# Hybrid decoder trunk: the later convolution's product and taps written behind the gate group's first subtraction

## The chip, the cores and the metric

The kernel runs on one core of a Trainium2 chip. The core has five engines that run side by side and wait for each other through semaphores: TensorE (PE, matmuls into the accumulation banks PSUM), VectorE (DVE), ScalarE (ACT), GpSimd (POOL) and SyncE (SP). DMAs are issued from the queues of SyncE, ScalarE and GpSimd. The metric is the time of the whole kernel in device microseconds; 1647.53 us is the median of three runs of the kernel before (1644.74 to 1648.75).

## What is computed

Two layers (D_MODEL 2048, 512 tokens, float32). Each normalises the input, projects it once into all heads, mixes in three branches and projects back:

```python
h = _rmsnorm(x, norm_g)
proj = h @ w_in
y_conv = _short_conv(cv_h, cv_b, cv_c, conv_w, conv_b) * silu(cv_g)   # b * (conv3(c * h) + bias)
...                                                                  # stick-breaking attention, linear attention
mix = jnp.concatenate([y_conv, y_sb, y_gla], axis=-1)
return x + mix @ w_out
```

The change concerns the first branch: the product c * h, and the causal convolution of width 3 over the tokens, which is done with three taps per channel.

## The kernel before

**Column groups.** The input projection is cut into groups of 256 columns, listed in `specs`, and worked off in that order; `cursor` counts them. The convolution has 512 channels, done as two convolutions of 256: conv 0 early in the layer, conv 1 last of all input groups. Each has four groups, in the order h, c, g, b. Behind "conv b 1" come the eight groups of the output projection.

**Weights.** `fetch(i)` (L362) loads a group's 2 MB of weights into one of two staging buffers `st`, from GpSimd's queue. ScalarE takes sums of squares (L383), GpSimd adds them over the partitions (L399), and VectorE makes a scale of them (L402 to L417). The weights are then split into a high and a low half in 16 bits: for a plain group ScalarE makes `wh` (L454) and VectorE `wl` (L461), in two halves of the depth. Each product is three matmuls: high by high, high by low, low by high.

**Quick groups.** The groups named in `QUICK_IN`, "conv c 1" and "conv g 1" among them, are done by `project_quick` with seven products of quarter blocks instead of eight. Their seven weight sums are made in `wsums` (L507 on ScalarE, L508 on VectorE; the seventh pair is `w7h`, `w7l`). The products go into two banks: pa and pb in one, pd and pf in the other, 24 matmuls each; in code order w11, wT2, w22, wT3, w21, wt1, wT4, where wT4 is the seventh weight and adds to pd. Between them ScalarE copies a partial result (L808, L812, L815) and VectorE adds and subtracts (L809, the first subtraction, then L816 to L821). wT4 may start only when L812 has read pd.

**conv 1.** `conv_in(1, go)` projects h into `hb` (L1198) and c into `uc`, multiplies c by its scale and by `hb` (L1203, once for each 128 channels, in place in `uc`), and makes `y` with the last tap and the bias (L1213) and the two earlier taps (L1215). `conv_out` projects the gate (group g) with `project_gate`, multiplies `y` by it (L1222), takes the largest value for a scale (`weight_ratio`), projects b with `project_cols` (L701 to L703) and multiplies by that (L1237).

**What stands beside it.** The last attention pair ends at the same time, spread out through `go`: `scores(1)` makes the weights of four query blocks (scans L1280, L1282), splits them (L1285 on ScalarE, L1286 on VectorE) and sends them through DMA transposes on SyncE's queue (L1288); `values` multiplies them with v (L1304) and applies the gate (L1308). `mixload` loads the finished parts of the mix back from DRAM (L923), the high half and then the low half, also on SyncE's queue; `weight_ratio` then brings all parts to one scale (L1188 on ScalarE, L1189 on VectorE), and the first output group multiplies them (L712 to L714).

**What sets the order.** The kernel is written through a scheduler that simulates the engines and puts each engine's instructions in the order in which they get ready there, by priority and by the place in the code. `order(a, b)` ties a behind b in that order without a wait on the chip. Only the opening of the kernel is in an order written by hand.

Of the kernel before, what the change touches and what calls it, by code (L numbers as in the profile page):

```python
# [11 lines left out]
ALU = mybir.AluOpType  # L12
# [31 lines left out]
def hybrid_trunk(ctx, tc, x, norm_g, w_in, conv_w, conv_b, sb_qn_g, sb_kn_g,  # L44
# [132 lines left out]
    def pcol(k, i):  # L177
        return par[:, base[k] + i:base[k] + i + 1]
# [506 lines left out]
    for l in range(depth):  # L685
# [89 lines left out]
                parts.extend([a[:, 2 * n], a[:, 2 * n + 1]] for n in range(2))  # L775
            return sums_of((xh, xl), parts, lambda t: [wk([P, HK, P], tag) for tag in ("zw", "zw", "g")])

        def project_quick(src, sums, y, cols):

            (w11, wT2, w22, wT3, w21, wt1, wT4), u = weights()  # L780
            (pa, pb), (pd, pf) = ([bk[:, n * GW:(n + 1) * GW] for n in range(2)]
                                  for bk in [bank(psp, "p") for _ in range(2)])
            a11, a12, a22 = ([a[:, 2 * r:2 * r + 2, c::2, :] for a in src] for r, c in ((0, 0), (0, 1), (1, 1)))
            s_, a21_22, a12_s, a11_21 = sums

            def prod(o, w, a, start, stop=False):
                for t in range(1 if cols else 2):
                    for kk in range(HK):
                        for i, (p_, q_) in enumerate(((0, 0), (0, 1), (1, 0))):
                            st_ = start and t == kk == i == 0  # L790
                            en = stop and kk == HK - 1 and i == 2
                            if cols:
                                mm = T.matmul(o, w[q_][:, kk, :], a[p_][:, :, kk, :], start=st_, stop=en,  # L793
                                              skip_group_check=True)
# [12 lines left out]
            hook(prod(pb, wT2, s_, False))  # L807
            S.activation(y12, za, AF.Copy)  # L808
            V.tensor_tensor(y21, zb, y12, ALU.subtract)  # L809
            prod(pf, w22, a12_s, True)  # L810
            prod(pd, wT3, a11_21, False)
            S.activation(y22, zd, AF.Copy)  # L812
# [3 lines left out]
            V.tensor_tensor(y12, zb, y12, ALU.subtract)  # L816
# [7 lines left out]
        def project(cols, dst):  # L824
# [4 lines left out]
            for _, u in project_quick((xh, xl), insums, y, cols):  # L829
                pass  # L830
            if cols:
                return [y[:, c, :] for c in range(2)], u
            return [y[:, 2 * b:2 * b + 2, :].rearrange("p a c -> p (a c)") for b in range(2)], u
# [13 lines left out]
                ps.append(o)  # L847
                yield t, o, u

        def project_gate(mx=None, logistic=False, room=None):  # L850
# [7 lines left out]
            ps, u = project(True, dst)  # L858
            quick_ = bool(g)
            g = dst() if not quick_ else g[0]  # L860
            top = sm(2, "gtop2") if mx is not None else None
            for c in range(2):
                y = g[:, c, :]
                if logistic:
                    a = wk([P, seq], "ga") if quick_ else y
                    tables.append(S.activation(a, ps[c], AF.Sigmoid, scale=u))
                    for b in tables[-9:-1]:
                        order(tables[-1], b)
                    if mx is None:
                        V.scalar_tensor_tensor(y, ps[c], u, a, ALU.mult, ALU.mult)  # L870
# [322 lines left out]
        def conv_in(j, then=lambda: None):  # L1193
# [5 lines left out]
            then()  # L1199
            uc = wk([P, 2, seq], "raw", 1) if j else wk([P, 2, seq], "zw")  # L1200
            ps, u = project(True, lambda: uc)
            for c in range(2):
                V.scalar_tensor_tensor(uc[:, c, :], ps[c], u, hb[:, c, :], ALU.mult, ALU.mult)  # L1203
            if j:
                mixload()
            y = wk([P, 2, seq], "kT")
            for c in range(2):
                ch = 2 * j + c

                def w_(i):  # L1210
                    return pcol("cw", (l * 3 + i) * 4 + ch)

                V.tensor_scalar(y[:, c, :], uc[:, c, :], w_(2), pcol("cb", l * 4 + ch), ALU.mult, ALU.add)  # L1213
                for d in (1, 2):
                    V.scalar_tensor_tensor(y[:, c, d:], uc[:, c, :seq - d], w_(2 - d), y[:, c, d:], ALU.mult, ALU.add)  # L1215
            then()
            return y, None if j else hb

        def conv_out(j, y, room, then=lambda: None):

            g, u = project_gate(logistic=j == 1, room=room)
            V.tensor_tensor(y, y, g, ALU.mult)  # L1222
            bound = sm(2, "cm")

# [249 lines left out]
```

## Time and profile before

| | |
|---|---|
| runs | 1644.74, 1647.53, 1648.75 us (median 1647.53) |
| profiled execution, its own time | 1652.09 us |
| its span, first to last instruction | 1650.3 us |
| TensorE busy | 1624.0 us (98%) |
| VectorE busy | 1418.1 us (86%) |
| ScalarE busy | 1184.7 us (72%) |
| granted TensorE clock | 1.0 |

The span is what the profile's times count from; the execution's own time is 1.8 us more. In a timeline a row gives the start, the duration, the engine, the line of the kernel, the operation with output and input, and in brackets how long the engine had been idle and what ended that. Matmuls overlap: a row's duration is longer than the distance to the next.

### The profile page before, as it was taken

What the parts mean: (1) busy time and instruction counts of PE and PEld (TensorE: products, weight loads), DVE (VectorE), ACT (ScalarE), POOL (GpSimd) and SP (SyncE); (2) the same over time, 40 slices, a digit from 0 to 9 for tenths busy, and PEclk for the clock granted to TensorE, in tenths of its full rate; (3) what the DMA queues carried; (4) which work ended last, traced back from release to release, by engine and by line L of the source; (5) the groups of instructions that cost most, each with busy time, mean ns of one, the idle gap of its engine ahead of it and who ended that gap; (6) DMA issues with size and microseconds to landing.
All of it is one profiled execution on the core that took longest, in us unless ns stands there. A gap on an engine that the chain in (4) does not pass through costs nothing.

```text
span 1650.3 us, 41605 instructions
## 1 busy us (share of the span) xinstructions
PE 1624.0 (98%) x17914; PEld 1342.5 (81%) x17914; DVE 1418.1 (86%) x2377; ACT 1184.7 (72%) x1743; POOL 265.8 (16%) x298
## 2 busy tenths in 40 slices
PE   8999999999999999999999999999999999999999
PEld 6746668989999967799986468689898989668998
DVE  7977989989898978898699689898898889888893
ACT  7667887877777776756766687787777768666571
POOL 0121011111112121111112011221121111211110
PEclk9999999999999999999999999999999999999999
DMA  7144334486768687544633344445776886894441
GB/s 259 54 146 127 73 113 100 116 161 149 166 148 167 148 167 207 161 154 150 204 110 116 103 116 112 132 94 137 152 157 153 151 163 152 165 189 157 154 155 53
DMA packets 193913, 234.90 MB, mean 142 GB/s; under 512 B 90226, under 2 KB 154044, under 8 KB 193216
## 3 DMA queue, kind: packets, MB, share of 16 engines
q0 software_dynamic: 76992, 177.22, 40.5%
q1 hardware_dynamic: 107728, 45.56, 14.5%
q10 hardware_dynamic: 9008, 9.45, 1.7%
q8 instruction: 140, 2.29, 0.6%
q14 instruction: 45, 0.37, 0.1%
HBM read 179.65 MB, written 14.68 MB: 118 GB/s over the span
## 4 chain that ended last, share of the span: by engine, by line
PE 37%; DVE 6%; DMA 4%; ACT 2%; issue 1%; POOL 0%; SPq 0%; DVEq 0%; ACTq 0%; POOLq 0%
PE psp L796 10%; PE psp L793 6%; PE psp L843 5%; PE psp L712 3%; PE psp L714 3%; PE psp L713 3%; PE psp L701 2%; PE psp L702 2%; PE psp L703 2%; DMA st<-in_w_in_dram 2%; DVE wl L508 1%; DMA m<-mixd 1%; DMA th<-za 1%; DVE za L1280 1%; DMA kT<-raw 1%
## 5 line engine op out<-in xcount | busy, mean ns | idle before, releaser
L507 ACT ACTIVATE wh<-st,ws 128x1024 f16<-128x1024 f32 x252 | 280.8, 1145 | 174.5 <-DVE st L527 92.0
L508 DVE SCALAR_TENSOR_TENSOR wl<-st,ws,wh 128x1024 f16<-128x1024 f32 x252 | 316.7, 1278 | 31.1 <-ACT wh L507 31.0
L383 ACT ACTIVATE junk<-st 128x2048 uint8<-128x2048 f32 x150 | 285.4, 1903 | 17.9 <-DMA st<-in_w_in_dram 8.8
L793 PE MATMUL psp<-s,wh 128*128 128x256 f16 x1152 | 195.6, 273 | 0.0
L793 PEld LDWEIGHTS <-wh 128*128 128x128 f16 x1728 | 168.3, 98 | 21.5 <-issue 1.3
L796 PE MATMUL psp<-wh,s 128*128 128x128 f16 x2048 | 176.9, 219 | 1.9 <-issue 1.9
L714 PE MATMUL psp<-wh,m 128*128 128x256 f16 x640 | 174.5, 273 | 1.2 <-DVE m L1189 1.2
L712 PE MATMUL psp<-wh,m 128*128 128x256 f16 x640 | 174.5, 273 | 0.2 <-issue 0.2
L796 PEld LDWEIGHTS <-s 128*128 128x128 f16 x3072 | 172.9, 98 | 2.0 <-issue 2.0
L713 PE MATMUL psp<-wl,m 128*128 128x256 f16 x640 | 174.5, 273 | 0.0
L796 PE MATMUL psp<-wl,s 128*128 128x128 f16 x1024 | 173.2, 219 | 0.0
L461 DVE SCALAR_TENSOR_TENSOR wl<-st,ws,wh 128x2048 f16<-128x2048 f32 x68 | 158.9, 2346 | 14.6 <-ACT wh L454 13.8
L454 ACT ACTIVATE wh<-st,ws 128x2048 f16<-128x2048 f32 x66 | 130.5, 1995 | 40.7 <-DVE ws L415 22.6
L362 POOL DMA_DIRECT2D st<-in_w_in_dram x114 | 109.8, 1029 | 297.8 <-DVE w7l L508 110.7
L793 PE MATMUL psp<-s,wl 128*128 128x256 f16 x576 | 156.7, 273 | 0.0
L796 PEld LDWEIGHTS <-m 128*128 128x128 f16 x2304 | 131.1, 98 | 2.7 <-issue 2.2
L399 POOL PARTITION_ALL_REDUCE wgm<-wm x75 | 55.5, 740 | 482.5 <-ACT junk L383 469.4
L386 POOL DMA_DIRECT2D st<-st x34 | 54.0, 1589 | 307.2 <-ACT junk L383 266.8
L793 PEld LDWEIGHTS <-wl 128*128 128x128 f16 x864 | 84.5, 98 | 13.4 <-issue 3.4
L796 PE MATMUL psp<-wh,m 128*128 128x128 f16 x1024 | 91.5, 219 | 0.4 <-DVE kT L809 0.4
L796 PE MATMUL psp<-wl,m 128*128 128x128 f16 x512 | 87.5, 219 | 0.0
L703 PEld LDWEIGHTS <-wl 128*128 128x128 f16 x448 | 43.8, 98 | 53.6 <-DVE wl L461 2.3
(442 smaller groups left out, 4199.8 us busy)
## 6 DMA issues: line engine op xcount, KB each, us to landing
st<-in_w_in_dram POOLq DMA_DIRECT2D x114, 1024.0 KB, 8.3
st<-in_w_out_dram POOLq DMA_DIRECT2D x32, 1024.0 KB, 8.5
st<-st POOLq DMA_DIRECT2D x34, 512.0 KB, 6.8
st<-in_w_in_dram SPq DMA_DIRECT2D x6, 1024.0 KB, 12.0
mixd<-g POOLq DMA_DIRECT2D x20, 256.0 KB, 7.9
x<-in_x_dram SPq DMA_DIRECT2D x4, 1024.0 KB, 4.9
qT<-in_x_dram ACTq DMA_DIRECT2D x8, 512.0 KB, 6.2
qT<-xs ACTq DMA_DIRECT2D x8, 512.0 KB, 4.0
```

The costliest lines, as they stand in the source:

```text
L362: load = queue.dma_start(s_, src[l, h * HK * P:(h + 1) * HK * P, c0:c0 + GW].rearrange("(k p) n -> p k n", p=P), max_dma_last_dim=1024)
L383: sq = S.activation(junk(HK * GW).rearrange("p (k n) -> p k n", k=part.shape[1]), part, AF.Square, accum_out=peak[i][:, h:h + 1])
L454: hi = S.activation(wh[:, :, :GW], staged[i][h], AF.Copy, scale=scales[i])
L461: V.scalar_tensor_tensor(wl[:, :, :GW], staged[i][h], scales[i], wh[:, :, :GW], ALU.mult, ALU.subtract)
L507: hi = S.activation(h_, b, AF.Copy, scale=sc)
L508: V.scalar_tensor_tensor(l_, b, sc, h_, ALU.mult, ALU.subtract)
L712: T.matmul(o, ah[:, t, k, :], wh[:, kk, :n], start=st_, stop=False, skip_group_check=True)
L713: T.matmul(o, ah[:, t, k, :], wl[:, kk, :n], start=False, stop=False, skip_group_check=True)
L714: return T.matmul(o, al[:, t, k, :], wh[:, kk, :n], start=False, stop=en, skip_group_check=True)
L793: mm = T.matmul(o, w[q_][:, kk, :], a[p_][:, :, kk, :], start=st_, stop=en, skip_group_check=True)
L796: mm = T.matmul(o[:, t * P:(t + 1) * P], a[p_][:, t, kk, :], w[q_][:, kk, :], start=st_, stop=en, skip_group_check=True)
L843: mm = T.matmul(o[:, :n], a_[:, t, k, :], w[k // HK][part][:, k % HK, :n], start=i == 0 and k == 0, stop=i == 2 and k == KT - 1)
```

## The change

For conv 1 alone, the product L1203 and the taps are put into a function `taps`, which `project_quick` calls through `mid` right behind the first subtraction L809 of the gate group, and the product is tied behind that subtraction. conv 0 calls `taps` where the code stood. Lines behind the change shift by 2 to 19 (L809 keeps its number; L1203 becomes L1210, L1213 L1219, L1215 L1221).

```diff
@@ -775,7 +775,7 @@
-        def project_quick(src, sums, y, cols):
+        def project_quick(src, sums, y, cols, mid=None):
...
@@ -806,7 +806,9 @@
             S.activation(y12, za, AF.Copy)
-            V.tensor_tensor(y21, zb, y12, ALU.subtract)
+            a = V.tensor_tensor(y21, zb, y12, ALU.subtract)
+            if mid is not None:
+                mid(a)
             prod(pf, w22, a12_s, True)
...
@@ -1199,26 +1201,43 @@
             then()
             uc = wk([P, 2, seq], "raw", 1) if j else wk([P, 2, seq], "zw")
             ps, u = project(True, lambda: uc)
-            for c in range(2):
-                V.scalar_tensor_tensor(uc[:, c, :], ps[c], u, hb[:, c, :], ALU.mult, ALU.mult)
             if j:
                 mixload()
-            y = wk([P, 2, seq], "kT")
-            for c in range(2):
-                ch = 2 * j + c
...
-            then()
-            return y, None if j else hb
+
+            def taps(behind=None):
+                y = wk([P, 2, seq], "kT")
+                for c in range(2):
+                    a = V.scalar_tensor_tensor(uc[:, c, :], ps[c], u, hb[:, c, :], ALU.mult, ALU.mult)
+                    if behind is not None:
+                        order(a, behind)
+                for c in range(2):
+                    ch = 2 * j + c
...
+                    V.tensor_scalar(y[:, c, :], uc[:, c, :], w_(2), pcol("cb", l * 4 + ch), ALU.mult, ALU.add)
+                    for d in (1, 2):
+                        V.scalar_tensor_tensor(y[:, c, d:], uc[:, c, :seq - d], w_(2 - d), y[:, c, d:], ALU.mult,
+                                               ALU.add)
+                return y
+
+            if j:
+                then()
+                return taps, None
+            y = taps()
+            then()
+            return y, hb
...
-            g, u = project_gate(logistic=j == 1, room=room)
+            made = [None if j else taps]
+
+            def mid(behind):
+                made[0] = taps(behind)
+
+            g, u = project_gate(logistic=j == 1, room=room, mid=mid if j else None)
+            y = made[0]
             V.tensor_tensor(y, y, g, ALU.mult)
```

What it does to the order is the same in both layers; the rows here are those of layer 0.

VectorE, from the scans' end of the last attention weights to the gate group's first subtraction and on (raw is `uc`, kT is `y`, wq/ws/wu are the scale of conv b's weights, w7l the low half of the gate group's seventh weight, za/zw the attention weights, wl the low half of conv b's weights). The stretch before the change:

```order
L1203 SCALAR_TENSOR_TENSOR raw_9105<-raw_9105,wu_8961,qT_8918 128x512 x2
L1282 SCALAR_TENSOR_TENSOR zw_9375<-zw_9375,za_9374 128x383
L1213 TENSOR_SCALAR kT_9337<-raw_9105,par 128x512
L402 TENSOR_TENSOR wq_9446<-wgm_9447 128x1
L1213 TENSOR_SCALAR kT_9337<-raw_9105,par 128x512
L508 SCALAR_TENSOR_TENSOR w7l_9181<-st_8930,ws_9170,w7h_9180 128x1024
L809 TENSOR_TENSOR g_9387<-psp_9391,g_9387 128x256
L1215 SCALAR_TENSOR_TENSOR kT_9337<-raw_9105,par,kT_9337 128x511
L411 TENSOR_SCALAR wq_9446<-wq_9446 128x1
L1286 TENSOR_TENSOR za_9353<-zw_9354,za_9353 128x896
L1215 SCALAR_TENSOR_TENSOR kT_9337<-raw_9105,par,kT_9337 128x511
L1286 TENSOR_TENSOR za_9374<-zw_9375,za_9374 128x384
```

The same stretch after the change:

```order
L1301 SCALAR_TENSOR_TENSOR zw_9366<-zw_9366,za_9365 128x383
L402 TENSOR_TENSOR wq_9437<-wgm_9438 128x1
L411 TENSOR_SCALAR wq_9437<-wq_9437 128x1
L415 TENSOR_SCALAR ws_9442<-wq_9437 128x1
L417 TENSOR_SCALAR wu_9444<-wq_9437,inoff_156 128x1
L508 SCALAR_TENSOR_TENSOR w7l_9181<-st_8930,ws_9170,w7h_9180 128x1024
L809 TENSOR_TENSOR g_9378<-psp_9382,g_9378 128x256
L1210 SCALAR_TENSOR_TENSOR raw_9105<-raw_9105,wu_8961,qT_8918 128x512 x2
L1305 TENSOR_TENSOR za_9344<-zw_9345,za_9344 128x896
L1305 TENSOR_TENSOR za_9365<-zw_9366,za_9365 128x384
L1219 TENSOR_SCALAR kT_9456<-raw_9105,par 128x512 x2
L461 SCALAR_TENSOR_TENSOR wl_9447<-st_9106,ws_9442,wh_9446 128x8x256
```

The product and the taps went from ahead of w7l to behind L809, the scale of conv b's weights came ahead of w7l, and the first low half of conv b's weights (L461) came ahead of all taps but the first.

ScalarE at the same place (g is the gate group's result, wh the high half of conv b's weights, m the mix). The stretch before the change:

```order
L1285 ACTIVATE za_9353<-zw_9354 128x896
L1419 DMA qT_10036<-in_x_dram 128x4x256
L1285 ACTIVATE za_9374<-zw_9375 128x384
L812 ACTIVATE g_9387<-psp_9392 128x256
L454 ACTIVATE wh_9455<-st_9106,ws_9451 128x8x256
L454 ACTIVATE wh_9459<-st_9106,ws_9451 128x8x256
L912 ACTIVATE m_9329<-e_9600,bsmix_8003 128x4x128
L815 ACTIVATE g_9387<-psp_9391 128x256
```

The same stretch after the change:

```order
L1304 ACTIVATE za_9344<-zw_9345 128x896
L1304 ACTIVATE za_9365<-zw_9366 128x384
L454 ACTIVATE wh_9446<-st_9106,ws_9442 128x8x256
L454 ACTIVATE wh_9450<-st_9106,ws_9442 128x8x256
L814 ACTIVATE g_9378<-psp_9383 128x256
L1438 DMA qT_10036<-in_x_dram 128x4x256
L914 ACTIVATE m_9327<-e_9600,bsmix_8003 128x4x128
L817 ACTIVATE g_9378<-psp_9382 128x256
```

Both high halves of conv b's weights now stand ahead of the gate group's copy L812 (L814 after the change), which reads pd.

TensorE behind the values of the attention pair (psm, L1304; L1323 after the change). Before it goes on with the seventh weight, which adds to the bank psp_9392:

```order
L1304 MATMUL psm_9599<-th_9062,v_7716 128x128
L793 LDWEIGHTS w7h_9180
L793 MATMUL psp_9392<-x_185,w7h_9180 128x256
L793 LDWEIGHTS w7l_9181
L793 MATMUL psp_9392<-x_185,w7l_9181 128x256
L793 LDWEIGHTS w7h_9180
L793 MATMUL psp_9392<-x_186,w7h_9180 128x256
```

After, it goes on with the products of the other bank, psp_9382:

```order
L1323 MATMUL psm_9599<-th_9062,v_7716 128x128
L793 LDWEIGHTS wh_9178
L793 MATMUL psp_9382<-x_185,wh_9178 128x256
L793 LDWEIGHTS wl_9179
L793 MATMUL psp_9382<-x_185,wl_9179 128x256
L793 LDWEIGHTS wh_9178
L793 MATMUL psp_9382<-x_186,wh_9178 128x256
```

The 48 matmuls of w21 and wt1 (wh_9178, wl_9179) now stand ahead of all 24 of the seventh weight; before, ten of those stood ahead of them.

More of the change, by code (lines that the diff above doesn't have):

```diff
@@ L822, in project_quick, with project @@
             yield 2, u
-        def project(cols, dst):
+        def project(cols, dst, mid=None):
             if cursor[0] not in quick:
@@ L828, in project @@
             y = dst()
-            for _, u in project_quick((xh, xl), insums, y, cols):
+            for _, u in project_quick((xh, xl), insums, y, cols, mid=mid):
                 pass
@@ L848, in project_by_token, with project_gate @@
                 yield t, o, u
-        def project_gate(mx=None, logistic=False, room=None):
+        def project_gate(mx=None, logistic=False, room=None, mid=None):
             g = []
@@ L856, in dst @@
                 return g[0]
-            ps, u = project(True, dst)
+            ps, u = project(True, dst, mid)
             quick_ = bool(g)
@@ L1201, in conv_in, with w_, conv_out @@
             ps, u = project(True, lambda: uc)
-            for c in range(2):
-                V.scalar_tensor_tensor(uc[:, c, :], ps[c], u, hb[:, c, :], ALU.mult, ALU.mult)
             if j:
                 mixload()
-            y = wk([P, 2, seq], "kT")
-            for c in range(2):
-                ch = 2 * j + c
[L1210 to L1215, printed above, removed]
-            then()
-            return y, None if j else hb
-        def conv_out(j, y, room, then=lambda: None):
-            g, u = project_gate(logistic=j == 1, room=room)
+            def taps(behind=None):
[6 more added lines that the diff above has]
+                    ch = 2 * j + c
+                    def w_(i):
+                        return pcol("cw", (l * 3 + i) * 4 + ch)
+                    V.tensor_scalar(y[:, c, :], uc[:, c, :], w_(2), pcol("cb", l * 4 + ch), ALU.mult, ALU.add)
[7 more added lines that the diff above has]
+            y = taps()
+            then()
+            return y, hb
+        def conv_out(j, taps, room, then=lambda: None):
+            made = [None if j else taps]
[3 more added lines that the diff above has]
+            y = made[0]
             V.tensor_tensor(y, y, g, ALU.mult)
```

## The prediction

> **What bounds the kernel now.** I read the head of the page first, then the list of waits of TensorE in the two stretches where the moved instructions stand (600 to 720 us for layer 0, 1410 to 1530 us for layer 1), then the timeline of each engine there.
>
> ```profile
> PE 1624.0 (98%) x17914; PEld 1342.5 (81%) x17914; DVE 1418.1 (86%) x2377; ACT 1184.7 (72%) x1743; POOL 265.8 (16%) x298
> ```
>
> TensorE is busy for 98% of the span, so a change on another engine pays only where it removes a wait of TensorE. The list of waits has one such wait in layer 0 and three in layer 1; of the three the longest is this last one here:
>
> ```profile
> PE psp L793 <- DVE w7l L508: 1.1, 1, 1.1
> ...
> PE psp L714 <- DVE m L1189: 1.2, 1, 1.2
> ```
>
> The timeline of TensorE shows all four in their places (start, duration, engine, line; in brackets the idle time ahead of the row and what ended it):
>
> ```profile
> 642.08 0.66 PE L1304 MATMUL psm<-th,v 128*128 128x256 f16 x6
> 642.61 0.27 PE L793 MATMUL psp<-x,w7h 128*128 128x256 f16 x1
> 643.97 0.28 PE L793 MATMUL psp<-x,w7l 128*128 128x256 f16 x1 [1.08 <-DVE w7l L508]
> ...
> 1453.81 0.71 PE L1304 MATMUL psm<-th,v 128*128 128x128 f16 x7
> 1454.88 0.27 PE L793 MATMUL psp<-m,w7h 128*128 128x256 f16 x1 [0.36 <-ACT g L812]
> 1456.03 0.28 PE L793 MATMUL psp<-m,w7l 128*128 128x256 f16 x1 [0.87 <-DVE w7l L508]
> ...
> 1487.04 0.27 PE L713 MATMUL psp<-wl,m 128*128 128x256 f16 x1
> 1488.51 0.28 PE L714 MATMUL psp<-wh,m 128*128 128x256 f16 x1 [1.20 <-DVE m L1189]
> ```
>
> Matmuls of this kind start 0.11 us apart (row with 96 of them below), so what a wait costs is the distance of two starts less 0.11. In layer 0 the second w7 matmul is 643.97 - 642.61 - 0.11 = 1.25 us late, for the low half of the gate group's seventh weight (w7l, L508). In layer 1 the same place loses 1456.03 - 1454.88 - 0.11 = 1.04 us, and the first w7 matmul comes 0.49 late: in layer 0 it starts 0.13 ahead of the modelled end of L1304 (642.08 + 0.66), which here would be 1453.81 + 0.71 - 0.13 = 1454.39. That is 1.53 us together. At 1488.51 the first output projection loses 1488.51 - 1487.04 - 0.11 = 1.36 us for the low half of the mix, which VectorE scales (L1189).
>
> **Why w7l is late.** VectorE's timeline:
>
> ```profile
> 639.88 1.39 DVE L1203 SCALAR_TENSOR_TENSOR raw<-raw,wu,qT 128x512 f32<-128x512 f32 x2
> ...
> 1451.93 1.39 DVE L1203 SCALAR_TENSOR_TENSOR raw<-raw,wu,qT 128x512 f32<-128x512 f32 x2
> 1453.23 0.55 DVE L1282 SCALAR_TENSOR_TENSOR zw<-zw,za 128x383 f32<-128x383 f32 x1
> 1453.70 0.54 DVE L1213 TENSOR_SCALAR kT<-raw,par 128x512 f32<-128x512 f32 x1
> 1454.16 0.15 DVE L402 TENSOR_TENSOR wq<-wgm 128x1 f32<-128x1 f32 x1
> 1454.69 1.28 DVE L508 SCALAR_TENSOR_TENSOR w7l<-st,ws,w7h 128x1024 f16<-128x1024 f32 x1
> 1455.88 0.42 DVE L809 TENSOR_TENSOR g<-psp,g 128x256 f32<-128x256 f32 x1
> 1456.94 1.08 DVE L1286 TENSOR_TENSOR za<-zw,za 128x896 f16<-128x896 f32 x1
> 1458.60 0.55 DVE L1286 TENSOR_TENSOR za<-zw,za 128x384 f16<-128x384 f32 x1
> 1461.95 4.61 DVE L461 SCALAR_TENSOR_TENSOR wl<-st,ws,wh 128x2048 f16<-128x2048 f32 x2 [0.63 <-ACT wh L454]
> ```
>
> VectorE has no gap here. Ahead of w7l stand the two multiplications by c (L1203, 1.39 us as a pair) and two first taps (L1213, 0.54 each; one row shown), none of which TensorE needs soon. Layer 1 repeats layer 0 812.05 us later (1451.93 - 639.88), so layer 0 is read off the same rows.
>
> **The change, part by part.** It adds and removes no instruction; it moves eight on VectorE in each layer (2 of L1203, 2 of L1213, 4 of L1215, all later), and the scheduler answers with moves of its own: on VectorE both L1286 come ahead of the taps, and L402 to L417, which make conv b's weight scale, ahead of w7l; on ScalarE conv b's two weight halves (L454) come ahead of the copy L812; and TensorE does the 48 matmuls of w21 and wt1 ahead of all 24 of w7. The rows for the new times:
>
> ```profile
> 639.54 0.61 POOL L399 PARTITION_ALL_REDUCE wgm<-wm  x1 [15.96 <-ACT junk L383]
> 1452.17 0.75 POOL L399 PARTITION_ALL_REDUCE wgm<-wm  x1 [16.79 <-ACT junk L383]
> 1456.27 1.79 POOL L362 DMA_DIRECT2D st<-in_w_out_dram  x2 [3.35 <-DVE w7l L508]
> 1466.86 1.76 POOL L362 DMA_DIRECT2D st<-in_w_out_dram  x2 [8.80 <-DVE wl L461]
> ...
> 1453.99 0.57 ACT L1285 ACTIVATE za<-zw 128x384 f16<-128x384 f32 x1
> 1454.40 0.43 ACT L812 ACTIVATE g<-psp 128x256 f32<-128x256 f32 x1
> 1459.91 3.90 ACT L454 ACTIVATE wh<-st,ws 128x2048 f16<-128x2048 f32 x2 [5.08 <-DVE ws L415]
> ...
> 1168.86 10.48 PE psp L793 x96
> ```
>
> 1. *w7l.* In layer 1 L1282 takes L1203's place and is through at 1451.93 + 0.47 = 1452.40. L402 then waits for GpSimd's sum, which ends at 1452.17 + 0.75 = 1452.92; four one-column instructions of at most 0.2 us each (0.15 in the row) bring w7l to a start of 1453.7 and an end of 1455.0, against 1455.97 before. In layer 0 the sum ends at 640.15, ahead of L1282's end, and w7l ends near 642.5 instead of 643.9. TensorE now wants it only behind 48 matmuls, 48 x 10.48 / 96 = 5.24 us: at 642.61 + 5.24 = 647.85 and 1454.39 + 5.24 = 1459.63. Both waits for w7l go, with 4 us to spare.
>
> 2. *The copy L812*, for which the first w7 matmul waited 0.49 us. It now queues behind L454's pair: L1285 ends at 1454.56, the pair takes 3.90, the copy 0.43, which gives 1458.9. Without the 48 matmuls in between that would cost 4.5 us; with them the copy is 0.7 us ahead of the 1459.63 at which it is wanted. In layer 0, where L1285 ends at 1454.56 - 812.05 = 642.5, the same sum gives 646.8 against 647.85, so 1.0 to spare. The cover is the 48 matmuls alone; what is missing of it is paid in full. I take nothing.
>
> 3. *conv b's low weight half* (L461, 2.3 us each), wanted by conv b's third matmul, 72 matmuls behind 1454.39, that is 1462.25. Behind w7l come L809 (0.42), the L1203 pair (1.39), L1286 (1.08 and 0.55), the L1213 pair (1.08) and L461: 1455.0 + 0.42 + 1.39 + 1.63 + 1.08 + 2.3 = 1461.8 at the most. It fits, by 0.4. Before, L461 started only at 1461.95 and the scheduler filled in with one matmul of L1304. The other taps, which ran ahead of L461 before, now stand between its halves and behind them.
>
> ```profile
> 1467.14 0.41 DVE L816 TENSOR_TENSOR g<-psp,g 128x256 f32<-128x256 f32 x1
> ...
> 1475.80 1.22 DVE L1222 TENSOR_TENSOR kT<-kT,g 128x1024 f32<-128x1024 f32 x1
> ```
>
> The taps' result is wanted at L1222 only, 8 us after the last of them. But L816, which reads the bank that conv b's second column group needs, now stands behind L1308, three taps and L913 (0.7 each, half a L1203 pair) and the second L461: 1461.8 + 5 x 0.7 + 2.3 + 0.41 = 1468.0 for its end. TensorE comes to that bank after 30 matmuls of twice the width, an estimate of 30 x 0.22 = 6.6 us behind 1462.25, at 1468.8. It fits, by 0.8.
>
> 4. *DMAs.* The staging buffer's release follows w7l, so the 2 MB load of output weights (L362, 1456.27, 0.3 us behind w7l) is issued about 1.0 us earlier, and the next one (1466.86, behind L461) about 2 us earlier. On SyncE's queue the long transpose comes ahead of the short one and waits for L1286: 1457.7 instead of 1457.27 at the worst. This reaches the fourth wait:
>
> ```profile
> 1457.27 1.23 SPq L1288 DMA_TRANSPOSE th<-za  x1
> 1458.60 9.33 SPq L1288 DMA_TRANSPOSE th<-za  x1
> 1468.02 2.19 SPq L1288 DMA_TRANSPOSE th<-za  x1
> 1470.30 0.53 SPq L923 DMA_DIRECT2D m<-mixd  x1
> ...
> 1470.89 17.06 DMA m<-mixd
> ...
> 1487.97 2.40 DVE L1189 TENSOR_SCALAR m<-m,ratio 128x1024 f16<-128x1024 f16 x6 [1.54 <-DMA m<-mixd]
> ...
> m<-mixd SPq DMA_DIRECT2D x2, 768.0 KB, 13.2
> ...
> 671.53 3.41 DVE L1189 TENSOR_SCALAR m<-m,ratio 128x1024 f16<-128x1024 f16 x7
> ```
>
> In layer 1 the three transposes hold SyncE's queue until 1470.2, then the low half of the mix is loaded, 17.06 us, and VectorE, which is idle, takes it at 1487.97. In layer 0 the same load takes 13.2 us, and VectorE finds it there at 671.53 without a wait. So layer 0's gain passes this place, and in layer 1 a TensorE that comes 1.53 us earlier stands there 1.53 us longer unless the load lands earlier too. The load's bounds: 0.4 us later (the transpose's wait) to 1.0 us earlier or more (everything ahead of it in the DMAs moved by w7l's 1.0), and in a run in which layer 1 loads like layer 0 there is no wait at all.
>
> **Sum.** Layer 0: -1.25. Layer 1: between 0 (the load lands as before) and -1.53 (it doesn't hold TensorE); I take the middle, -0.77, since the two layers' rows for the same load disagree and lie on either side. Together -2.0 us, with ends at -0.85 (layer 1 loses 0.4) and -2.8. Behind the output projections nothing is moved. The profiled execution took 1652.09 us with a span of 1650.3, 4.6 above the median of the runs, 1647.53; the terms are differences, so I take them off the median: 1645.5. What a measurement of this kernel can tell from no change is about 0.3%, 4.9 us; the runs alone spread over 1644.74 to 1648.75.
>
> **Rivals.**
> - *The load eats more.* Layer 1 gives nothing and loses up to 0.4: 1646.3 to 1646.7. For it speaks that VectorE is idle until 1487.97 with its other inputs ready; against it that what is ahead of the load was started earlier.
> - *All four waits go.* The load lands 2.9 us earlier, as a load of 13.2 us would: -1.25 - 1.53 - 1.36 = -4.1, 1643.4. For it speaks layer 0 alone.
> - *The output weights push ahead, slower.* The second 2 MB load is issued 2 us earlier, so more of it is moved while the transposes and the low half of the mix wait. At this rate
>
> ```profile
> DMA packets 2607, 4.00 MB, mean 334 GB/s; under 512 B 500, under 2 KB 2036, under 8 KB 2607
> ```
>
>   (the DMA view of 1478 to 1490 us) 1 MB is 3.1 us and the whole load 6.3. One half ahead of the mix costs layer 1 3.1, less layer 0's 1.25: 1649.4, no change that shows. Both ahead give 6.3 - 1.25 = +5.0: 1652.6, slower. It decides from 6.2 us of delay on. Against it: 2 us earlier at 334 GB/s is 0.7 MB, a third of the load.
>
>   The Trainium skill, page "DMA: Bandwidth & Descriptors", section "Issuing engines are not separate DMA queues", says that DMAs begun by ScalarE, SyncE or GpSimd all end on the same 16 engines and interleave. By that rule the earlier load shares instead of passing, which is the milder form of this rival; the trace agrees as far as both queues move data in the 1478 to 1490 window.
>
> **How the numbers follow.** Forecast 0.60, the load eats more 0.22, all four go 0.08, output weights ahead 0.10. All but the last rival's hard form lie within 4.9 us of 1647.53. Faster by over 0.3% needs all four waits and a low median: 0.07. Slower by over 0.3% is the hard form and a high median: 0.07. Same: 0.86. The range goes from 1642.5 (all four, and 0.9 below for the runs' spread) to 1650.0 (one half of the weights ahead, 1649.4, and 0.6).
>
> **What the changed profile would show.** Right: no wait of line 793 for w7l in either layer; TensorE going from L1304 straight to w21; the L812 copy ending near 1458.9 less what layer 0 gained, ahead of the first w7 matmul; a wait of L714 in layer 1 longer than 1.2 us. Wrong: the first w7 matmul waits for the L812 copy (ScalarE's pair slower or started late), conv b's third matmul waits for L461, or VectorE waits for the mix in layer 0 as well.

## The result, and the profile after

The changed kernel is slower: 1674.97 us, median of five runs (1674.71 to 1678.72), against 1646.35 us for the kernel before on the same chip (1644.74 to 1648.75). The ratio is 1.0163, 95% interval 1.013 to 1.0195. The forecast was 1645.5 us, range 1642.5 to 1650.0. The profiled execution took 1677.98 us with a span of 1676.2 us, 25.9 more than the span before.

The list of waits of TensorE, first for 600 to 720 us (layer 0, two rows), then for 1420 to 1530 us (layer 1). The columns are the wait and what ended it, then us in total, how often, and the longest:

```profile
PE psp L714 <- DVE m L1191: 5.2, 2, 4.6
PE psp L712 <- DVE kT L1256: 1.5, 1, 1.5
...
PE psm L1323 <- DMA th<-za: 10.4, 3, 6.6
PE psp L714 <- DVE m L1191: 5.8, 1, 5.8
PE psp L793 <- DVE g L809: 1.3, 1, 1.3
```

Both waits for w7l are gone, as forecast. In their place TensorE waits for data that DMAs bring: for the transposed attention weights (th) and, through VectorE, for the low half of the mix (m). The stretches of 40 us show how much that is. Columns: busy time and count of instructions of PE, PEld, DVE, ACT and POOL, then the granted clock, the DMA share and GB/s. First two stretches of the kernel before:

```profile
640.00:680.00 40.00, 38.92 (x268) 25.46 (x267) 32.72 (x57) 28.11 (x31) 6.48 (x9) 1.00 0.91 264
...
1480.00:1520.00 40.00, 38.80 (x337) 32.31 (x336) 35.17 (x52) 25.55 (x25) 5.45 (x7) 1.00 0.54 171
```

and the same and their neighbours after the change:

```profile
640.00:680.00 40.00, 34.72 (x225) 21.20 (x223) 27.57 (x49) 24.39 (x25) 6.42 (x9) 0.96 1.04 242
680.00:720.00 40.00, 38.51 (x335) 33.63 (x336) 32.41 (x41) 20.63 (x20) 2.58 (x4) 0.95 0.34 101
...
1480.00:1520.00 40.00, 23.74 (x128) 14.04 (x127) 14.16 (x27) 14.93 (x16) 2.15 (x3) 0.74 0.76 151
```

In the last stretch TensorE is idle for 16.3 of 40 us instead of 1.2, and its mean granted clock is 0.74 instead of 1.00. The mean hides where the clock was low. Two stretches of 10 us, and two matmuls from TensorE's timeline:

```profile
1500.00:1510.00 10.00, 3.05 (x14) 1.57 (x13) 0.49 (x1) 0.00 (x0) 0.00 (x0) 0.50 0.89 256
...
1520.00:1530.00 10.00, 10.00 (x94) 8.96 (x92) 9.34 (x11) 3.59 (x3) 0.40 (x1) 1.00 0.01 2
...
1512.71 0.42 PE L713 MATMUL psp<-wl,m 128*128 128x256 f16 x1
1512.93 0.42 PE L714 MATMUL psp<-wh,m 128*128 128x256 f16 x1
```

It is low around the waits, and most of that time TensorE is idle anyway. Behind the last wait, from 1512.32 to 1516.56 us, 20 matmuls follow each other 0.21 us apart instead of 0.11, an estimate of 20 x 0.10 = 2 us. The loss can be laid on the layers by VectorE's w7l, which is made at the start of each stretch (before, then after the change; the row of layer 1 before, 1454.69, stands in the prediction):

```profile
642.63 1.28 DVE L508 SCALAR_TENSOR_TENSOR w7l<-st,ws,w7h 128x1024 f16<-128x1024 f32 x1
```

```profile
641.28 1.27 DVE L508 SCALAR_TENSOR_TENSOR w7l<-st,ws,w7h 128x1024 f16<-128x1024 f32 x1
...
1460.31 1.27 DVE L508 SCALAR_TENSOR_TENSOR w7l<-st,ws,w7h 128x1024 f16<-128x1024 f32 x1
```

VectorE gets to layer 0's w7l 1.4 us earlier than before. From there to layer 1's it takes 1460.31 - 641.28 = 819.03 us instead of 812.06, 7.0 lost. From there to the end it takes 215.9 instead of 195.6, 20.3 lost. The sum is the 25.9.

What is late is seen on the two queues that issue the DMAs. SP's rows are the transposes of the last head's weights, one long and two short; a merged row with x2 or x3 goes from the first one's start to the last one's end, and the row of 660.15 is the last of the three above it. POOL's rows are the two halves of the second output group's weights, 2 MB. First layer 0 of the kernel before, then both layers after the change:

```profile
654.92 1.76 POOL L362 DMA_DIRECT2D st<-in_w_out_dram  x2 [8.93 <-DVE wl L461]
...
654.77 1.21 SPq L1288 DMA_TRANSPOSE th<-za  x1
```

```profile
652.86 1.76 POOL L362 DMA_DIRECT2D st<-in_w_out_dram  x2 [8.22 <-DVE wl L461]
...
645.24 16.25 SPq L1307 DMA_TRANSPOSE th<-za  x3
660.15 1.33 SPq L1307 DMA_TRANSPOSE th<-za  x1
...
1471.77 1.76 POOL L362 DMA_DIRECT2D st<-in_w_out_dram  x2 [8.10 <-DVE wl L461]
...
1464.27 16.07 SPq L1307 DMA_TRANSPOSE th<-za  x2
1480.44 4.82 SPq L1307 DMA_TRANSPOSE th<-za  x1
...
1485.94 25.81 DMA m<-mixd
```

In layer 0 that load is now issued at 652.86 and the last transpose at 660.15, 7.3 us behind it. Before, the load was issued at 654.92, 0.15 us behind the last transpose (654.77). In layer 1 the last transpose is 8.7 us behind the load, against 1468.02 - 1466.86 = 1.2 before. Part of that distance is already the loss: the transposes hold SyncE's queue longer, so the last one is issued later. The low half of the mix is behind the transposes on SyncE's queue; its largest part, 768 KB, then takes 25.81 us to land in layer 1, against 17.06.

The DMA view tells what happens between. Its first row gives, for 40 slices of the window, the time of the packets that start in the slice as a share of the 16 DMA engines, in tenths. The rows of queues give packets, MB and that share for the whole window; q1 is SyncE's queue (the transposes and the mix), q0 GpSimd's (the weights). For 657 to 664 us, layer 0 after the change:

```profile
DMA  9990000000000000000000053999999999979999
...
DMA packets 411, 0.25 MB, mean 35 GB/s; under 512 B 353, under 2 KB 379, under 8 KB 411
...
q1 hardware_dynamic: 377, 0.12, 105.7%
q0 software_dynamic: 33, 0.13, 5.1%
```

A 0 says that hardly a packet starts in that slice, not that the engines are free: packets that started before are still open. With 2 MB of weights issued and waiting, 0.25 MB is moved in 7 us. The weights move as if on one engine alone: 33 packets, 5.1% of 16 engines (0.8 of one), and 0.13 MB, a sixteenth of the 2 MB.

The single packets in the trace show it closer. From 657.57 us on, 16 packets of 4096 bytes of the weights, together a sixteenth of one 1 MB half, are moved one at a time, 0.17 to 0.18 us each; the last ends at 661.03. All that time 22 packets of 256 bytes on SyncE's queue, begun from 656.70 to 657.44, stay open; they end together, from 661.18 to 661.41.

For 1477 to 1489 us of layer 1 after the change, and then 1469 to 1477 us of the kernel before, which has the same thing in layer 1 at length (in layer 0 for 1 to 2 us):

```profile
DMA packets 626, 0.76 MB, mean 63 GB/s; under 512 B 451, under 2 KB 473, under 8 KB 626
```

```profile
DMA packets 941, 0.51 MB, mean 64 GB/s; under 512 B 855, under 2 KB 874, under 8 KB 941
```

### The profile page after: what moved, and what is told of

The parts are those of the page before. It is cut to its first block, busy times and chain, and to the rows that moved or that the text cites. A ratio compares the mean times of both kernels' runs of the same rounds, so it can differ in the third digit from the quotient of the medians.

```text
span 1676.2 us, 41608 instructions
## 1 busy us (share of the span) xinstructions
PE 1628.8 (97%) x17914; PEld 1344.5 (80%) x17914; DVE 1418.1 (85%) x2377; ACT 1184.7 (71%) x1743; POOL 263.4 (16%) x298
## 4 chain that ended last, share of the span: by engine, by line
PE 38%; DMA 5%; DVE 5%; ACT 2%; issue 1%; POOL 0%; SPq 0%; ACTq 0%; DVEq 0%; POOLq 0%
PE psp L796 10%; PE psp L793 6%; PE psp L845 4%; PE psp L714 3%; PE psp L712 3%; PE psp L713 3%; PE psp L701 2%; PE psp L702 2%; PE psp L703 2%; DMA m<-mixd 2%; DMA st<-in_w_in_dram 1%; DMA th<-za 1%; DVE wl L508 1%; DMA kT<-raw 1%; DVE w7l L508 1%
## 5 line engine op out<-in xcount | busy, mean ns | idle before, releaser
L793 PE MATMUL psp<-s,wh 128*128 128x256 f16 x1152 | 195.6, 273 | 0.0
L714 PE MATMUL psp<-wh,m 128*128 128x256 f16 x640 | 176.7, 276 | 11.0 <-DVE m L1191 11.0
L712 PE MATMUL psp<-wh,m 128*128 128x256 f16 x640 | 176.9, 276 | 1.5 <-DVE kT L1256 1.5
L461 DVE SCALAR_TENSOR_TENSOR wl<-st,ws,wh 128x2048 f16<-128x2048 f32 x68 | 159.1, 2347 | 13.3 <-ACT wh L454 12.9
L454 ACT ACTIVATE wh<-st,ws 128x2048 f16<-128x2048 f32 x66 | 130.7, 1997 | 28.6 <-DVE ws L415 14.0
```

The costliest lines, as they stand in the source:

```text
L454: hi = S.activation(wh[:, :, :GW], staged[i][h], AF.Copy, scale=scales[i])
L461: V.scalar_tensor_tensor(wl[:, :, :GW], staged[i][h], scales[i], wh[:, :, :GW], ALU.mult, ALU.subtract)
L712: T.matmul(o, ah[:, t, k, :], wh[:, kk, :n], start=st_, stop=False, skip_group_check=True)
L714: return T.matmul(o, al[:, t, k, :], wh[:, kk, :n], start=False, stop=en, skip_group_check=True)
```

## The experiments

Three theories at the start. **A**: the second output group's weights, issued 2 us earlier by the change, get to the DMA engines ahead of the last transposes, and the two hold each other up. **B**: the residual load of the second output group (512 KB of the input that its result is added to, ScalarE's queue, L1438), which the change moves from ahead of the stretch into it, is one queue too many. **C**: the order of the transposes on SyncE's queue (the long one ahead of both short ones, instead of between them). Every kernel is the changed one with one edit, unless it says otherwise, and is compared with the kernel before on the same chip.

### The residual loads later

```diff
         while later:
             go()
+        gate_end = tables[-1]
...
-            S.dma_start(rt, res_src[:, gi * GW:(gi + 1) * GW].rearrange("(t p) c -> p t c", p=P))
+            res = S.dma_start(rt, res_src[:, gi * GW:(gi + 1) * GW].rearrange("(t p) c -> p t c", p=P))
+            if not gi:
+                order(res, gate_end)
```

> The changed kernel with one load moved: the first output group's residual load, on ScalarE's queue, is tied behind the gate's second sigmoid, some 15 us later, out of the stretch in which the mix and the output weights are loaded. (On SyncE's queue the scheduler then puts the short transpose ahead of the long one, as before the change.) Theory A, the second output-weight load, now issued 2 us earlier, is in the DMA engines when the transposes want them: nothing gained, 1668 to 1678 us. Theory B, the residual load, which the change brings into that stretch as a third queue, delays the mix and the transposes behind it: back to 1644 to 1652. Theory C, the order of the three transposes on SyncE's queue: also 1644 to 1652, as the next kernel.

Measured: 1658.03 us (1653.94 to 1664.91), ratio 1.0048 (1.0013 to 1.0084). The residual load is part of it: 17 of the 28.6 us come back. The edit names the first group's load, but the second group's stands behind it on the same queue, so both move: in layer 0 from 622.96 and 644.24 us to 657.12 and 657.79. That is not out of the way of the mix: the last part of its low half is issued at 658.25 and takes 26.4 us to land, and in layer 0 TensorE waits 6.4 us for the low half, through VectorE. So the run shows that the residual load's place matters, not how much of the loss is its own.

### The old order of the transposes

```diff
+                        to = th[hh][:, i, 7 * n:7 * n + zw // P, :]
+                        if j == 3 and hh and i and not n:
+                            held.append((to, part))
+                            continue
-                        nc.sync.dma_start_transpose(th[hh][:, i, 7 * n:7 * n + zw // P, :], part)
+                        a_ = nc.sync.dma_start_transpose(to, part)
+                        if held:
+                            order(nc.sync.dma_start_transpose(*held.pop()), a_)
```

> The changed kernel with the short transpose put back ahead of the long one on SyncE's queue, nothing else. Theory A (second output-weight load too early) and theory B (residual load): 1668 to 1678 us. Theory C (order of the transposes): 1644 to 1652.

Measured: 1676.2 us, ratio 1.018 (1.0151 to 1.021). The whole loss is still there, so the order alone (C) is out.

### The second output group's weights behind the mix

```diff
         queue = nc.gpsimd if i > 2 else nc.sync
+        if names[i] == "1":
+            queue, behind = nc.sync, mixlast[-1]
...
-                    order(nc.sync.dma_start(mix[i][:, :, ks, :], mixd[l][:, i * NT:(i + 1) * NT, ks, :]), lastmm[0])
+                    a = nc.sync.dma_start(mix[i][:, :, ks, :], mixd[l][:, i * NT:(i + 1) * NT, ks, :])
+                    order(a, lastmm[0])
+                    mixlast.append(a)
```

> The changed kernel with the load of the second output group's weights issued from SyncE's queue behind the low half of the mix instead of from GpSimd's, so that it cannot be ahead of the transposes or the mix. Theory A: the waits for the mix and for the transposes go, 1641 to 1648 us (before the change less the 2.8 us of the waits for w7l, and up to 1.4 for the mix). Theories B and C: the transposes are still late, 1660 to 1675.

Measured: 1643.4 us (1641.74 to 1646.18), ratio 0.9976 (0.9964 to 0.9989). The loss is gone, and the residual load is where the change put it. So without the early second weights the residual load costs nothing that shows.

### Plain copies in place of the transposes

The last head's weights are copied without being transposed; bytes, queue and place are the same.

```diff
+                        if j == 3 and hh:
+                            a_ = nc.sync.dma_start(to, part.rearrange("p (b c) -> p b c", c=P))
+                        else:
+                            nc.sync.dma_start_transpose(to, part)
```

> The changed kernel with the last attention head's four transposes per layer replaced by plain copies of the same bytes (the transposing is left out, so that head's values are others). All loads keep their order and their time of issue as far as the transposes let them. If it is the transposes that hold the DMA engines while a load is behind on one of them (theory A, and theory C in part): the stretch of 20 to 25 GB/s goes and the time is 1640 to 1650 us. If the loads alone are too much for the DMA engines there (theory B): 1660 us or more.

Measured: 1646.26 us, ratio 0.9996 (0.9984 to 1.0007). With the same loads in flight at the same place the loss is gone. The DMA view of 657 to 664 us, the window of layer 0 above:

```profile
DMA  9999998999997999999999899999999999999899
...
DMA packets 944, 2.47 MB, mean 353 GB/s; under 512 B 30, under 2 KB 494, under 8 KB 944
```

All engines are busy throughout, and ten times the bytes are moved. The early loads alone cost nothing; it takes the transposes beside them. The copies also move in larger packets (30 under 512 bytes of 944, against 353 of 411), so the run doesn't tell the transposing from the small packets that come with it.

### A tie that is no wait

The second output group's load was tied behind the last tap with `order`, from GpSimd to VectorE.

> The changed kernel with the second output group's load left on GpSimd's queue, but tied behind the last tap on VectorE, so that it is issued 2.6 us later (about 655.5 instead of 652.9 in layer 0); every engine's order is the same as in the changed kernel. Theory A in its sharp form (those 2 us decide): most of the loss goes, 1646 to 1654. Theory B: the residual load is as in the changed kernel, so the loss stays, 1668 to 1676. A third theory, D (any load that is still moving when the transposes get to the engines costs, and a later one as much as an earlier): 1668 to 1680.

Measured: 1677.86 us (two runs). The edit did not do what the expectation says. `order` sets the scheduler's order alone; across two engines it leaves no wait, and the orders were the same anyway. In layer 0 the load was issued 654.24 - 644.23 = 10.01 us behind the first group's, in the changed kernel 652.86 - 642.85 = 10.01. So this run is the changed kernel once more, and tells none of the theories apart.

### A real wait

Here GpSimd first clears one column of conv c's dead values, for which it has to wait until the last tap has read them.

```diff
+        if names[i] == "1":
+            behind = G.memset(dead_c[-1][:, 1, 0:1], 0.0)
         for h in range(2):
             s_ = whole[i][:, h * HK:(h + 1) * HK, :]
```

> The changed kernel with the second output group's load on GpSimd's queue behind a one-column memset of conv c's dead values, which waits for the last tap on VectorE, so the load is issued about 2.6 us later (near 655.6 in layer 0, behind the issue of the last short transposes, as before the change). On VectorE the first low half of the first output group's weights also comes about ten short instructions later. Theory A, sharp (the 2 us by which the change brings the load forward decide): 1645 to 1655. Theory D (not the time of issue but the number of loads that are moving when the transposes reach the engines decides, residual load, first and second output weights): the three are still there together, 1663 to 1678.

Measured: 1644.83 us (1642.88 to 1646.52), ratio 0.9986 (0.9976 to 0.9996). Queue, bytes and residual load are those of the changed kernel. The load is issued 655.47 - 642.19 = 13.28 us behind the first group's in layer 0, where it was 10.01, so the wait came to 3.3 us rather than 2.6; 30 us hang on it. Layer 0, the load on GpSimd's queue and the last transpose on SyncE's:

```profile
655.47 1.75 POOL L365 DMA_DIRECT2D st<-in_w_out_dram  x2 [0.56 <-issue]
...
655.29 2.01 SPq L1311 DMA_TRANSPOSE th<-za  x1
```

The load is behind the last transpose again, by 0.2 us, and TensorE has no wait at all in either stretch. In layer 1 it is still 1465.70 - 1463.78 = 1.9 us ahead of the last transpose, and that costs nothing either, so to be behind the last transpose is not what decides. The stretch at a low rate is still there, but short: 135 GB/s from 656 to 657 us and 51 from 657 to 658; the kernel before has 201 and 23 there. The DMA view of 658 to 665 us:

```profile
DMA packets 1825, 2.33 MB, mean 333 GB/s; under 512 B 1115, under 2 KB 1349, under 8 KB 1824
```

### Half the load

```diff
+            if names[i] == "1" and h:
+                queue, behind = nc.sync, late
             load = queue.dma_start(s_, src[l, h * HK * P:(h + 1) * HK * P, c0:c0 + GW].rearrange(
```

(`late` is the last load of the mix, as `mixlast[-1]` above.)

> The changed kernel with the second output group's weights in two parts: the first half (1 MB) issued from GpSimd's queue as in the changed kernel, the second half from SyncE's queue behind the mix's low half. If the engines are held for as long as the early bytes take at one engine's rate (about 20 GB/s in the collapse), half the bytes give half the loss, 14 of 28 us: 1655 to 1663. If any such load sets off the whole loss: 1668 to 1678. If a small one stays below what matters: 1643 to 1648.

Measured: 1653.54 us (1651.24 to 1655.11), ratio 1.004 (1.0025 to 1.0056). Half the early bytes cost about a quarter of the loss, a little less than expected for half. It is no matter of bytes alone: in layer 1 of this profile, 1465 to 1479 us, the rate is low for as long as in the changed kernel, with half the load, and TensorE waits 8.1 us for data of DMAs:

```profile
DMA packets 1193, 1.24 MB, mean 88 GB/s; under 512 B 923, under 2 KB 952, under 8 KB 1193
```

In layer 0 the stretch below 90 GB/s goes from 656 to 661 us, against 657 to 664 in the changed kernel, and TensorE has no wait there.

### The kernel before, with each of the two loads moved

First the residual load alone, put behind the first high half of conv b's weights:

```diff
-            S.dma_start(rt, res_src[:, gi * GW:(gi + 1) * GW].rearrange("(t p) c -> p t c", p=P))
+            res = S.dma_start(rt, res_src[:, gi * GW:(gi + 1) * GW].rearrange("(t p) c -> p t c", p=P))
+            if gi == 1:
+                order(res, his["conv b 1", 0])
```

> The kernel before with the second output group's residual load (512 KB) moved behind the first high half of conv b's weights on ScalarE, issued at 649.8 instead of 642 in layer 0, so that it runs beside the output weights and the mix as in the changed kernel; nothing else changed. Theory A: 1647 to 1650, since the second group's weights are issued as before. Theory B: most of the loss of the changed kernel shows, 1660 to 1676.

Measured: 1663.28 us, spread over 1648.31 to 1673.89, ratio 1.0097 (1.0056 to 1.0138). A alone is not the whole of it: with the second weights where they were before, the residual load in the stretch costs 16 us in the median, and from run to run anything between almost none and nearly all of the loss. And here the load is issued behind the last transpose in both layers (653.96 against 649.20 us, and 1469.53 against 1467.97). B is right in this kernel and wrong in the two above (weights behind the mix, and the real wait), where the residual load is in the stretch and costs nothing. Then the second weights alone, behind the mix (the same edit as above):

> The kernel before with the second output group's weights issued from SyncE's queue behind the mix's low half, nothing else changed. Theory A (the loss comes from the second group's weights reaching the DMA engines ahead of the last transposes): the 8 us at low rate that layer 1 has before (1469 to 1477) go, and with them the 1.2 us wait of L714 for the mix, so 1644 to 1646; what is left between this kernel and the changed one with the same edit (1643.4) is then the change's own worth, 1 to 2 us. Theory B (the residual load as a third queue): before, the residual load runs alone, so nothing changes, 1646.5 to 1648.

Measured: 1646.47 us (1643.17 to 1649.65), ratio 0.999 (0.9971 to 1.001); the wait of L714 for the mix is gone, and no gain of it shows in the time.

### The best version, and what the change is worth in it

Both edits of the changed kernel together, twice, and the kernel before with its second weights behind the mix once more:

> The changed kernel with both edits: the second output group's weights behind the mix's low half and the residual loads behind the gate's second sigmoid. Theory A: nothing is left for the second edit to repair, 1643 to 1644.5, equal to the first edit alone (1643.4). Theory B: 1 to 2 us below it, 1641.5 to 1642.5.

> The changed kernel with the second output group's weights behind the mix's low half and the residual loads behind the gate's second sigmoid, timed closely. By all theories as in its first run, 1642.6: 1641.5 to 1643.5, 0.2 to 0.35% faster than the kernel before.

> The kernel before with the second output group's weights behind the mix's low half, timed again on the same chip as the final version. If the change itself (VectorE's products and taps later) is worth the 2 us of the prediction once its transfers are out of the way, this kernel is 2 to 4 us slower than the final version: 1644.5 to 1647. If the gain came from the moved load alone, the two are equal, 1642.5 to 1643.5.

Measured: 1642.59 us (8 runs), ratio 0.9971 (0.996 to 0.9982), then on another chip 1643.75 us (11 runs), ratio 0.9984 (0.9975 to 0.9993), which is above the upper end of what was expected. The kernel before with its weights behind the mix took 1646.33 us there, ratio 0.9996 (0.9986 to 1.0005). Over both chips, by the runs' means, the changed code is 3.0 us faster than the old code (1.9 to 4.1) once the weights are behind the mix in both. So the moved taps are worth something; of the moved load by itself no gain shows. The two also differ in the place of the residual loads, so the 3.0 us are for both together; the run with the weights alone behind the mix (1643.4, ratio 0.9976) says about the same on a third chip. In the old code the two waits for w7l, 1.1 and 0.9 us, are still there. TensorE has no wait left between 600 and 720 us or between 1410 and 1530 us in this version. It beats both kernels, by 3 to 4 us of the one before.

## Why the prediction was wrong

**Steps 1 to 3 held.** Layer 1 of the changed kernel, VectorE, ScalarE and TensorE:

```profile
1465.54 2.35 DVE L461 SCALAR_TENSOR_TENSOR wl<-st,ws,wh 128x2048 f16<-128x2048 f32 x1
...
1464.94 0.42 ACT L814 ACTIVATE g<-psp 128x256 f32<-128x256 f32 x1
...
1461.98 0.27 PE L793 MATMUL psp<-m,wh 128*128 128x256 f16 x1 [1.33 <-DVE g L809]
1467.21 0.27 PE L793 MATMUL psp<-m,w7h 128*128 128x256 f16 x1
1470.27 0.38 PE L703 MATMUL psp<-m,wl 128*128 128x512 f16 x1
```

- *w7l* (step 1) ends at 641.28 + 1.27 = 642.55 in layer 0, forecast 642.5, and no matmul of w7 waits for it.
- *The copy* (now L814) ends at 1465.36, 1.85 us ahead of the first w7 matmul at 1467.21; 0.7 was forecast. The 48 matmuls do cover it.
- *conv b's low half* ends at 1467.89, 2.4 us ahead of the third matmul of conv b at 1470.27; 0.4 was forecast.
- One wait was overlooked there: w21 goes into the bank that L809 reads, and L809 still stands behind w7l. In layer 1 the first w21 matmul is 1.33 us late for it, nearly all of the 1.53 us that layer 1 had to gain. It is 1.0 us in the run with the weights behind the mix and does not show in the run with the real wait.

**Step 4 failed, the DMAs.** The time that the mix takes to land is the term that it had wrong. It bounded what the earlier loads do to the mix between 0.4 us later and 1.0 earlier, by their times of issue. The rival named the right load and the right direction, "the output weights push ahead", but priced it in bytes at 334 GB/s, at most 6.3 us, and put 0.10 on it. That rate is from 1478 to 1490 us, behind the transposes. Beside the transposes the rate of the same kernel is 64 GB/s (1469 to 1477 us), and after the change 35 and 63. The 17.06 us for 768 KB, quoted in the prediction, was the sign of it: at 334 GB/s that and the whole 2 MB are moved in 6.3 + 2.3 = 8.6. Measured, the same 768 KB took 25.81 us in layer 1, the transposes were late as well, and TensorE waited 10.4 us for them and 5.8 for the mix. The prediction's last sign of being wrong, VectorE waiting for the mix in layer 0 as well, is there too: 13.5 us of waits.

The Trainium skill, page "DMA: Bandwidth & Descriptors", section "Queues, rings and completion order", has each DMA engine take turns between its queues packet by packet. By that an earlier load shares the engines. The run with plain copies agrees (353 GB/s); beside the transposes the whole went at the pace of packets that stayed open, 3.8 to 4.6 us each in layer 0, where a transpose's packet of 256 bytes otherwise took 0.018.

**A move was left out.** The part of the document on the change shows the residual load (L1419, now L1438) going behind the two halves L454 on ScalarE, and no step of the prediction prices it. The rows of layer 0, before and after:

```profile
641.30 0.38 ACTq L1419 DMA_DIRECT2D qT<-in_x_dram  x1
...
644.24 0.41 ACTq L1438 DMA_DIRECT2D qT<-in_x_dram  x1
```

Before, it is issued 644.21 - 641.30 = 2.9 us ahead of the first output group's weights, and its packets are moved by 645 us. After, it is issued 644.24 - 642.85 = 1.4 us behind them, and its packets are moved from 648.6 to 657.1 us, beside those weights and the long transpose. It is no small term: 17 us come back when it is moved out of the changed kernel's stretch, and it costs 16 by itself in the kernel before.

**The rest of the sum was near.** With its transfers out of the way the change gives 3.0 us (1.9 to 4.1), where the sum said 2.0, and with the real wait alone 2.0 (1644.83 against 1646.85 on its chip). So the sum holds where the earlier load does no harm, and there only. That it came so near is in part luck: its term for layer 1, -0.77, was the middle between two bounds, and the wait for L809 was not in it.

**What stays open.** That the loss comes from the second weights being issued early, with the residual load beside them and transposes on the engines, is shown: take away the early issue or the transposes and it is gone. Why the packets stay open is argued. In layer 0 all fits one engine that is behind with its sixteenth of the weights while transposes keep the others waiting until it is through: the pace of one packet at a time, the 16 packets of a half, and the 22 open packets that end together right behind them. But the trace gives no engine to a packet, and in other places it is packets of the weights that stay open: up to 6.4 us in layer 1 of the changed kernel, 3.1 with the residual loads later, 3.7 in the kernel before with the residual load moved. With the plain copies no packet of SyncE's queue took over 0.8 us in either stretch. Nor is it shown why the residual load does harm in one place and none in another; and the second weights were not made earlier in the kernel before.

## What to carry to other kernels

When a change lets a load start earlier, look at what else is on the DMA queues from then on, a transpose above all, and price the load by the rate of that very stretch, not by a good stretch near it. Every DMA that the order moves is a term of the sum, also when it is far from its use. If an early load does harm, try it behind the urgent transfers on their own queue, or make it wait for real; both took the loss away here. An order between two engines that sets no semaphore does nothing on the chip.

## What the hardware showed that was not expected

- DMA transposes with loads from other queues in flight brought the rate of all queues down to 35 GB/s for 7 us in layer 0 and 63 GB/s for 12 us in layer 1, against 353 GB/s with plain copies of the same bytes (657 to 664 us). The engines were not idle: packets of 256 bytes stayed open for 3.8 to 4.6 us. The Trainium skill, page "DMA: Bandwidth & Descriptors", section "Rules for kernel authors", says in its row on transposes that corrupt each other's values that a transpose next to ordinary DMAs needs nothing. No run here says anything against that for the values; for the time the measurement decides, 1674.97 us against 1646.35.
- 3.3 us of difference in the issue of one load moved the time by 30 us (1674.97 and 1644.83), and half of the load moved back by about 21 (1674.97 and 1653.54).
- Around its waits TensorE was also slower: its granted clock was 0.50 from 1500 to 1510 us, where it was busy for 3.05 us, and 1.00 again from 1520 to 1530, where it was busy throughout.
